# Ten gate tiles and the stick-breaking queries and keys of block 1 computed by 512-column products

## The chip, the cores and the metric

The program runs on one core of one Trainium2 chip. The metric is the device time of one execution in microseconds (us); lower is better. The core's engines work side by side, each through its own list of instructions in order: TensorE (PE, with its weight loads as PEld), VectorE (DVE), ScalarE (ACT), GpSimd (POOL) and SyncE (SP, which issues nearly all the transfers here).

## The reference

Two transformer blocks follow each other on 256 tokens of width 2048, in float32. The change lies in the first one. What it computes, cut to what matters:

```python
h = rms_norm(x, norm_g)
proj = h @ w_in                       # 2048 -> 8192
qa, ka, va, ga, qb, kb, vb, gb = split(proj)      # 1024 columns each
# stick-breaking attention, 8 heads of 128, blocks of 128 queries
z = (qa_head @ ka_head.T) * 128 ** -0.5
log_stay = where(s < t, log_sigmoid(-z), 0)
after = reversed_cumsum(log_stay) - log_stay
w = where(s < t, exp(log_sigmoid(z) + after), 0)
ya_head = w @ va_head
# yb: chunk-band attention on qb, kb, vb (8 heads)
mixed = concat([ya * silu(ga), yb * silu(gb)])
x = x + mixed @ w_out
```

The second block (latent attention, window attention and a convolutional feed-forward network of width 5632) is not touched.

## The kernel before

**Numbers in two parts.** A float32 operand of a large product is split into two tiles of the matrix type: `hi`, its rounded value (ACT), and `lo`, the rest (DVE, input minus `hi`). A product of weights and activations is then three: whi·ahi, whi·alo, wlo·ahi. Activations stand transposed, 256 tokens in the free direction, so a group of three for one block of 128 input features has three moving operands of 256 columns; this is `wmm` (L267 to L272). The second block's up projection has another form, `wide` (L274 to L278): there ahi and alo lie side by side in one tile, whi·[ahi alo] is one product of 512 columns into a whole PSUM bank, wlo·ahi one of 256 columns into its left half, and the two halves are added when the bank is emptied (L1553, L1554). For a block of 128 features `wmm` has three weight loads and 768 columns, `wide` two weight loads and 768 columns.

**The stream.** `Stream` holds a list of chunks of weights, 1024 columns each, which is 8 blocks of 128. SP loads a chunk, ACT makes `whi` (L123), DVE makes `wlo` (L125), and PE multiplies. There are four buffers for `whi` and four for `wlo`: the split of a chunk waits until PE has done with the chunk four places earlier. Rows of the second block's `ada` matrix go through the same stream; each is one DVE instruction (L392) of 1024 columns.

**The order.** The orders of PE and SP are those in which the code is written. Each chunk ticks a clock twice, once before its products and once after half of them, and tasks on it (`spawn`, `step`, `tick`) put their next instructions there. The orders of ACT and DVE are made by the scheduler when the program is built. Every engine then keeps its order, whatever comes ready first.

**The part that changes.** `x_pair` makes 16 pairs `hx` of activation tiles. `first_gates` and `w_pair` compute 16 gate tiles, each 128 output columns by 256 tokens, two to a bank; `gate_handler` multiplies them by `rrep`, each token's reciprocal norm (L618, DVE), and applies Silu (ACT). The first four tiles share two banks of tag `s`. The other twelve are six pairs, four chunks each, in banks of tag `g`, of which there are three, taken in turn. Much later come the eight stick-breaking heads: for each, `w_pair` makes the queries and the keys in one bank (four chunks), and `stick_head` empties it with one DVE instruction into `qkT` (L764). Two ticks later, in the middle of the next chunk, PE multiplies queries and keys (L767, L768; "the scores" below), and DVE takes the result (L770). The sums over later positions (L781 to L783) of the head before stand in PE's order directly behind the bank's last product; their result is taken by L784.

Of the kernel before, what the change touches and what calls it, by code (L numbers as in the profile page):

```python
# [9 lines left out]
F32 = mybir.dt.float32  # L10
F32R = mybir.dt.float32r
I32 = mybir.dt.int32
AF = mybir.ActivationFunctionType
ALU = mybir.AluOpType

P = 128
T = 256
# [197 lines left out]
def two_blocks(ctx, tc, xT, cvec, cst, vecs, w1, wo1, bch, ada, wz, wv, wuq, wuk, wuv, bsw, wo2, wup, wdn, out):  # L215
# [3 lines left out]
    def pool(name, side=None):  # L219
        kw = {} if side is None else {"side": side}  # L220
        return tc.alloc_tile_pool(name=name, bufs=1, reuse_waits="tile", **kw)
# [5 lines left out]
    S = Stream(tc, wp)  # L227
# [9 lines left out]
    def C(name):  # L237
        o, w = CST[name]
        if o < NCST0:
            return cs0[:, o:o + w]  # L240
        if o < NCST1:
            return ns["cs1"][:, o - NCST0:o - NCST0 + w]
        return cs[:, o - NCST1:o - NCST1 + w]

    def V(name, a=0, b=None):
        o, w = VEC[name]
        return vv[:, o + a:o + (w if b is None else b)]
# [3 lines left out]
    def bank(tag):  # L251
        t = psum.tile([P, 512], F32, tag=tag, name=tag, bufs={"g": 3, "s": 2, "t": 2, "o": 1}[tag])
        return t

    def two(ap):
        return ap.rearrange("p (a t) -> p a t", a=2)

    def act(**kw):
        return nc.scalar.activation(**kw)

    tt = nc.vector.tensor_tensor
# [4 lines left out]

    def wmm(out, whi, wlo, a, first, last):  # L267

        ahi, alo = a
        mm(out, lhsT=whi, rhs=ahi, start=first, stop=False)  # L270
        mm(out, lhsT=whi, rhs=alo, start=False, stop=False)  # L271
        mm(out, lhsT=wlo, rhs=ahi, start=False, stop=last)  # L272

    def wide(out, whi, wlo, a, first, last):  # L274

        ahi, alo, both = a
        mm(two(out), lhsT=whi, rhs=both, start=first, stop=False)  # L277
        mm(out[:, :T], lhsT=wlo, rhs=ahi, start=False, stop=last)  # L278

    def wchunk(lst):  # L280

        def mms(hi, lo):
            def one(c, e):
                out, a, first, last = e() if callable(e) else e
                wmm(out, hi[:, c * P:(c + 1) * P], lo[:, c * P:(c + 1) * P], a, first, last)
            return [lambda c=c, e=e: one(c, e) for c, e in enumerate(lst)]
        return mms
# [65 lines left out]
    def at_once(gen):  # L353
        try:
            while True:
                next(gen)
        except StopIteration as e:
            return e.value
# [52 lines left out]
    def ada_rate(r, upto):  # L411

        ada_acc[1:] = [r, upto]
# [47 lines left out]
    ph = pool("ph", "right")  # L461
    pmx = pool("pmx")
    p1 = pool("p1")
    hx = []
# [5 lines left out]
    def x_pair(q):  # L470
        if q % 2 == 0:
            tag = ("qt", "kt", "v", "v")[q // 2]
            t = p1.tile([P, 2, 512], F32, tag=tag, name="x4", bufs=3 if tag == "v" else 1)
            x4.append(t.rearrange("p a (k t) -> p (a k) t", t=T))
        xq = x4[q // 2][:, 2 * (q % 2):2 * (q % 2) + 2]
        for j in range(2):
            if j == 0 or q == 0:
                n = 1 if q == 0 else 2
                nc.sync.dma_start(out=xq[:, j:j + n], in_=xT[:, 2 * q + j:2 * q + j + n, :])
                if q == 0:  # L480
                    S.load_to(j + 1)
            hi = ph.tile([P, T], F32R, tag="hx", name="hx", bufs=32)
            lo = ph.tile([P, T], F32R, tag="hx", name="hx", bufs=32)
            g = V("ng", 2 * q + j, 2 * q + j + 1)
            ns["hx"] = act(out=hi, in_=xq[:, j], func=AF.Copy, scale=g)
            stt(out=lo, in0=xq[:, j], scalar=g, in1=hi.bitcast(F32), op0=ALU.mult, op1=ALU.subtract)
            hx.append((hi, lo))
            if q == 0:
                with tc.issue_after(ns["hx"].ins):
                    S.split_one()  # L490

    rt = p1.tile([P, 2], F32, name="rt")
    rrep = p1.tile([P, T], F32, name="rrep")
    rrep2 = rrep.unsqueeze(1).to_broadcast([P, 2, T])
# [24 lines left out]
    def w_pair(srcs, acts, handler, n=16, per=8, tag="g"):  # L519

        box = {}
        flat = [(a, k) for a in range(2) for k in range(n)]
        for c in range(0, 2 * n, per):
            part = flat[c:c + per]

            def pre():
                box["ps"] = bank(tag)

            def entry(a, k):
                return lambda: (box["ps"][:, a * T:(a + 1) * T], acts()[k], k == 0, k == n - 1)  # L530
            S.chunk(srcs(c // per), len(part) * P, wchunk([entry(a, k) for a, k in part]),
                    pre=pre if c == 0 else None,
                    post=(lambda: handler(box["ps"])) if c + per >= 2 * n else None)

    def w_one(srcs, acts, handler, n=16, per=8):
        box = {}
# [59 lines left out]
    hxs = lambda: hx  # L596
    u = [0]

    def next_w1(n):
        b = u[0]  # L600
        u[0] += n
        return lambda c: w1[b + c]


    order = list(range(8, 16)) + list(range(8))
    gates = {}

    def gate_handler(j):
        def h(ps):
            at_once(evac(ps))  # L610

        def late(ps):
            S.spawn(evac(ps), 8)

        def evac(ps):
            for i in range(2):
                gt = pmx.tile([P, T], F32, tag="mh", name="gate", bufs=16)
                tt(out=gt, in0=ps[:, i * T:(i + 1) * T], in1=rrep, op=ALU.mult)  # L618
                last = act(out=gt, in_=gt, func=AF.Silu)
                gates[order[2 * j + i]] = gt  # L620
            if j == 7:
                with tc.issue_after(last.ins):
                    nc.scalar.preload_act_table_set("natural_log_exp_and_others")
            yield 1
        return evac if j < 2 else late if j == 2 else h


    gb = []
# [23 lines left out]
    for j in range(2, 8):  # L652
        if j == 2:
            ada_rate(0.52, 64)
        w_pair(next_w1(4), hxs, gate_handler(j))

    mixed = {}

# [100 lines left out]

    SB = (2,1,4,2,1,3)  # L760

    def stick_head(ps, h):
        qk = p1.tile([P, 512], F32, tag="qkT", name="qkT", bufs=2)
        tt(out=two(qk), in0=two(ps), in1=rrep2, op=ALU.mult)  # L764
        yield SB[0]
        sc = bank("s")
        mm(sc[:, 0:256], lhsT=qk[:, 256:384], rhs=qk[:, 0:256], start=True, stop=True)  # L767
        mm(sc[:, 256:384], lhsT=qk[:, 384:512], rhs=qk[:, 128:256], start=True, stop=True)  # L768
        zm = p1.tile([P, 384], F32, tag="zm", name="zm", bufs=2)
        stt(out=zm, in0=sc[:, :384], scalar=128.0 ** -0.5, in1=C("msb"), op0=ALU.mult, op1=ALU.add)  # L770
        yield SB[1]
        e = p1.tile([P, 384], F32, tag="e", name="e", bufs=3)
        act(out=e, in_=zm, func=AF.Abs)
        act(out=e, in_=e, func=AF.Exp, scale=-1.0)
        act(out=e, in_=e, func=AF.Ln, bias=1.0)
        yield SB[2]
        sp = p1.tile([P, 384], F32, tag="sp", name="sp", bufs=2)
        stt(out=sp, in0=zm, scalar=0.0, in1=e, op0=ALU.max, op1=ALU.add)
        yield SB[3]
        cum = bank("s")  # L780
        mm(cum[:, 0:256], lhsT=C("tri"), rhs=sp[:, 0:256], start=True, stop=False)  # L781
        mm(cum[:, 128:256], lhsT=ones, rhs=sp[:, 256:384], start=False, stop=True)
        mm(cum[:, 256:384], lhsT=C("tri"), rhs=sp[:, 256:384], start=True, stop=True)  # L783
        tt(out=zm, in0=zm, in1=cum[:, :384], op=ALU.subtract)  # L784
        yield SB[4]
        w = p1.tile([P, 384], F32, tag="pT", name="pT", bufs=2)
        act(out=w, in_=zm, func=AF.Exp)
        yield SB[5]
        o = bank("o")
        hs = slice((h % 4) * 128, (h % 4 + 1) * 128)  # L790
        vt = qkv["va%d" % (h // 4)]
        attend(o, vt[:, 0, hs], vt[:, 1, hs], w)
        yield from finish_head(o, h)

    last_head = []
    for h in range(8):
        def handler(ps, h=h):
            t = S.spawn(stick_head(ps, h))
            S.step(t)
            last_head.append(t)  # L800
        w_pair(next_w1(4), hxs, handler)


    warm = small.tile([P, 2], F32, name="warm")
# [70 lines left out]
    for n, (j, a, hf) in enumerate(seq):  # L875
# [4 lines left out]
        def pre(j=j, a=a, hf=hf):  # L880
            if j not in banks1:
                banks1[j] = bank("g")
            if hf == 1 and "pu" not in ns:
                start_u()

        def entry(j, a, i):
            return lambda: (banks1[j][:, a * T:(a + 1) * T], mixed[order[i]], i == 0 and a == 0, i == 15 and a == 1)
        S.chunk(wo1[(2 * j + a) * 2 + hf], 1024, wchunk([entry(j, a, hf * 8 + i) for i in range(8)]), pre=pre,
                post=(lambda j=j: out1_handler(j)) if (a, hf) == (1, 1) else None)
# [864 lines left out]
```

## Time and profile before

| | us |
|---|---|
| median of 3 runs | 1886.03 |
| lowest and highest | 1885.96, 1886.21 |
| the profiled execution's own time | 1886.98 |
| its span in the trace | 1885.2 |

The profile is of one execution. Its span runs from the first to the last instruction of the program; about 1.8 us of the execution's own time lie around it. Engines' busy times overlap. A matmul's bar in the trace is longer than its share of PE, because matmuls are pipelined: the cost of one is the distance from its start to the start of the next. In the rows, "idle before" is how long an engine stood still before an instruction and the name behind the arrow is what ended it.

### The profile page before, as it was taken

The page shows a single profiled execution, that of the slowest core. Times are in us where ns is not written, and L with a number is a line of the kernel's source. Part 1 is how long each engine was busy: PE and PEld are TensorE (multiplying, and loading weights), DVE is VectorE, ACT ScalarE, POOL GpSimd, SP SyncE. Part 2 cuts the span into 40 slices and gives each one's busy share as a digit, 9 for nine tenths or more (in the row PEclk, how much of TensorE's full clock was granted, in tenths as well). Part 3 has the DMA queues.
Part 4 walks back from the last instruction along what each step waited for, and adds up shares of the span by engine and source line. Part 5 has one row for each costly group of instructions (what it writes and reads, how often), then busy time and mean ns, then how long its engine had stood idle before and what let it go on. Part 6 is the DMA issues. An engine that isn't in the chain of part 4 may idle for free.

```text
span 1885.2 us, 31970 instructions
## 1 busy us (share of the span) xinstructions
PE 1873.0 (99%) x12144; PEld 1704.0 (90%) x12144; DVE 1360.2 (72%) x2219; ACT 1015.4 (54%) x1650; POOL 188.6 (10%) x298
## 2 busy tenths in 40 slices
PE   9999999999999999999999999999999999999998
PEld 9988889999999999999999889888888888888886
DVE  7777877767787777777878766988888777644444
ACT  7445454444565555555566558555555555543442
POOL 0001120000125233330022100000000000000000
PEclk9999999999999999999999999999999999999999
DMA  9888777658688777768655664877777666656663
GB/s 357 300 278 298 248 264 262 239 188 266 196 302 278 256 256 265 261 209 270 214 175 176 236 223 160 266 245 251 249 247 245 191 190 190 190 179 190 190 190 123
DMA packets 128169, 438.92 MB, mean 233 GB/s; under 512 B 14352, under 2 KB 20368, under 8 KB 127760
## 3 DMA queue, kind: packets, MB, share of 16 engines
q1 hardware_dynamic: 127872, 436.88, 70.3%
q8 instruction: 95, 1.56, 0.3%
q14 instruction: 58, 0.48, 0.1%
q10 hardware_dynamic: 144, 0.01, 0.0%
HBM read 434.73 MB, written 2.10 MB: 232 GB/s over the span
## 4 chain that ended last, share of the span: by engine, by line
PE 97%; ACT 1%; DVE 1%; DMA 0%; POOL 0%; issue 0%; SPq 0%; DVEq 0%; POOLq 0%
PE g L277 16%; PE g L270 12%; PE g L272 12%; PE g L271 12%; PE g L278 8%; PE g L294 7%; PE g L295 7%; PE g L293 7%; PE s L293 3%; PE s L294 3%; PE s L295 3%; PE o L457 1%; PE t L450 1%; PE s L1132 1%; PE o L458 1%; PE s L272 1%
## 5 line engine op out<-in xcount | busy, mean ns | idle before, releaser
L125 DVE TENSOR_TENSOR wlo<-raw,whi 128x1024 fp32r<-128x1024 f32 (+2 forms) x623 | 762.6, 1225 | 383.8 <-ACT whi L123 376.1
L123 ACT ACTIVATE whi<-raw 128x1024 fp32r<-128x1024 f32 (+2 forms) x623 | 652.1, 1049 | 615.0 <-PE g L271 145.9
L277 PE MATMUL g<-h,whi 128*128 128x512 f32 x1344 | 466.1, 392 | 0.0
L278 PE MATMUL g<-h,wlo 128*128 128x256 f32 x1344 | 376.3, 280 | 0.0
L277 PEld LDWEIGHTS g<-h,whi 128*128 128x128 f32 x1344 | 252.3, 188 | 56.4
L270 PE MATMUL g<-h,whi 128*128 128x256 f32 x880 | 253.0, 288 | 0.0
L278 PEld LDWEIGHTS g<-h,wlo 128*128 128x128 f32 x1344 | 252.7, 188 | 0.0
L272 PE MATMUL g<-h,wlo 128*128 128x256 f32 x880 | 247.2, 281 | 0.0
L271 PE MATMUL g<-h,whi 128*128 128x256 f32 x880 | 247.2, 281 | 0.0
L392 DVE SCALAR_TENSOR_TENSOR raw<-raw,crep 128x1024 f32<-128x1024 f32 x192 | 239.0, 1245 | 1.6 <-DMA raw<-in_ada_dram 1.2
L271 PEld LDWEIGHTS g<-h,whi 128*128 128x128 f32 x880 | 166.0, 189 | 0.0
L270 PEld LDWEIGHTS g<-h,whi 128*128 128x128 f32 x880 | 166.0, 189 | 0.0
L272 PEld LDWEIGHTS g<-h,wlo 128*128 128x128 f32 x880 | 165.8, 188 | 0.0
L270 PE MATMUL g<-hx,whi 128*128 128x256 f32 x448 | 127.7, 285 | 0.0
L272 PE MATMUL g<-hx,wlo 128*128 128x256 f32 x448 | 125.8, 281 | 0.0
L271 PE MATMUL g<-hx,whi 128*128 128x256 f32 x448 | 125.8, 281 | 0.0
L293 PE MATMUL g<-whi,hx 128*128 128x512 f32 x256 | 104.6, 409 | 0.0
L295 PE MATMUL g<-whi,hx 128*128 128x512 f32 x256 | 101.0, 395 | 0.0
L294 PE MATMUL g<-wlo,hx 128*128 128x512 f32 x256 | 101.0, 395 | 0.0
L270 PEld LDWEIGHTS g<-hx,whi 128*128 128x128 f32 x448 | 84.5, 189 | 0.1
L271 PEld LDWEIGHTS g<-hx,whi 128*128 128x128 f32 x448 | 84.5, 189 | 0.1
L272 PEld LDWEIGHTS g<-hx,wlo 128*128 128x128 f32 x448 | 84.4, 188 | 0.0
(344 smaller groups left out, 3520.0 us busy)
## 6 DMA issues: line engine op xcount, KB each, us to landing
raw<-in_ada_dram SPq DMA_DIRECT2D x192, 512.0 KB, 4.4
raw<-in_wup_dram SPq DMA_DIRECT2D x176, 512.0 KB, 4.3
raw<-in_w_dram SPq DMA_DIRECT2D x127, 512.0 KB, 4.8
raw<-in_wz_dram SPq DMA_DIRECT2D x122, 512.0 KB, 4.6
raw<-in_wdn_dram SPq DMA_DIRECT2D x88, 512.0 KB, 3.6
raw<-in_wo_dram SPq DMA_DIRECT2D x64, 512.0 KB, 4.1
raw<-in_wuq_dram SPq DMA_DIRECT2D x24, 384.0 KB, 3.7
raw<-in_wuv_dram SPq DMA_DIRECT2D x8, 512.0 KB, 4.5
```

The source lines that it names most:

```text
L123: nc.scalar.activation(out=hi[:, :n], in_=raw, func=AF.Copy)
L125: last = nc.vector.tensor_tensor(out=lo[:, :n], in0=raw, in1=hi[:, :n].bitcast(F32), op=ALU.subtract)
L270: mm(out, lhsT=whi, rhs=ahi, start=first, stop=False)
L271: mm(out, lhsT=whi, rhs=alo, start=False, stop=False)
L272: mm(out, lhsT=wlo, rhs=ahi, start=False, stop=last)
L277: mm(two(out), lhsT=whi, rhs=both, start=first, stop=False)
L278: mm(out[:, :T], lhsT=wlo, rhs=ahi, start=False, stop=last)
L293: mm(out, lhsT=ahi[:, t], rhs=hi[:, w], start=first, stop=False)
L294: mm(out, lhsT=ahi[:, t], rhs=lo[:, w], start=False, stop=False)
L295: mm(out, lhsT=alo[:, t], rhs=hi[:, w], start=False, stop=last)
L392: stt(out=raw, in0=raw, scalar=1.0, in1=crep_now[0][:, h * 1024:(h + 1) * 1024], op0=ALU.mult, op1=ALU.mult, accum_out=modh[:, k:k + 1])
L450: nc.tensor.transpose(pt[:, j * P:(j + 1) * P], e[:, j * P:(j + 1) * P], ident)
```

## The change

The two parts of `hx` become the halves of one tile. A new `w_side` computes one output tile over two chunks by `wide`, in a bank of its own. A new `halves` empties such a bank: ACT copies its right half, DVE adds the left half to that. Of the six gate pairs, the first stays with `w_pair` and the other five become ten tiles of `w_side`, each emptied by ACT copy, DVE add, DVE multiplication by `rrep` and ACT Silu. The queries and the keys of a stick-breaking head become two `w_side` tiles; each is copied, added and multiplied into its half of `qkT`. The number and the order of chunks, and the ticks, are as before; so are the chunk-band products and values, which read `hx` as weights.

```diff
     def wmm(out, whi, wlo, a, first, last):
-        ahi, alo = a
+        ahi, alo = a[:2]
...
-            hi = ph.tile([P, T], F32R, tag="hx", name="hx", bufs=32)
-            lo = ph.tile([P, T], F32R, tag="hx", name="hx", bufs=32)
+            both = ph.tile([P, 2, T], F32R, tag="hx", name="hx", bufs=16)
+            hi, lo = both[:, 0], both[:, 1]
...
-            hx.append((hi, lo))
+            hx.append((hi, lo, both))
...
+    def w_side(srcs, acts, handler):
+        box = {}
+        for c in range(2):
+            def pre():
+                box["ps"] = bank("g")
+            def mms(hi, lo, c=c):
+                def one(j):
+                    k = c * 8 + j
+                    wide(box["ps"], hi[:, j * P:(j + 1) * P], lo[:, j * P:(j + 1) * P], acts()[k], k == 0, k == 15)
+                return [lambda j=j: one(j) for j in range(8)]
+            S.chunk(srcs(c), 1024, mms, pre=pre if c == 0 else None,
+                    post=(lambda: handler(box["ps"])) if c == 1 else None)
+
+    def halves(dst, ps):
+        act(out=dst, in_=ps[:, T:], func=AF.Copy)
+        tt(out=dst, in0=ps[:, :T], in1=dst, op=ALU.add)
...
+    def side_gate(i):
+        def h(ps):
+            gates[order[i]] = gt = pmx.tile([P, T], F32, tag="mh", name="gate", bufs=16)
+            halves(gt, ps)
+            tt(out=gt, in0=gt, in1=rrep, op=ALU.mult)
+            last = act(out=gt, in_=gt, func=AF.Silu)
...
     for j in range(2, 8):
-        w_pair(next_w1(4), hxs, gate_handler(j))
+        if j == 2:
+            w_pair(next_w1(4), hxs, gate_handler(j))
+        else:
+            for i in (2 * j, 2 * j + 1):
+                w_side(next_w1(2), hxs, side_gate(i))
...
-    def stick_head(ps, h):
-        qk = p1.tile([P, 512], F32, tag="qkT", name="qkT", bufs=2)
-        tt(out=two(qk), in0=two(ps), in1=rrep2, op=ALU.mult)
+    def stick_head(qk, h):
         yield SB[0]
...
+        def handler(ps, h=h, a=0, box=box):
+            if a == 0:
+                box["qk"] = p1.tile([P, 512], F32, tag="qkT", name="qkT", bufs=2)
+            qk = box["qk"][:, a * T:(a + 1) * T]
+            halves(qk, ps)
+            tt(out=qk, in0=qk, in1=rrep, op=ALU.mult)
+            if a == 1:
+                t = S.spawn(stick_head(box["qk"], h))
+                S.step(t)
+                last_head.append(t)
+        for a in range(2):
+            w_side(next_w1(2), hxs, lambda ps, a=a, h=handler: h(ps, a=a))
```

The change also gives DVE and ACT another order. Three places follow; in each row stand line, operation, the tile written, behind `<-` the tiles read, and the written shape.

**The first head, DVE.** The order of before, from the split of the chunk ahead of the bank's end to the taking of the scores (`zm`):

```order
L125 TENSOR_TENSOR wlo<-raw,whi 128x1024
L764 TENSOR_TENSOR qkT<-g,rrep 128x512
L125 TENSOR_TENSOR wlo<-raw,whi 128x1024
L392 SCALAR_TENSOR_TENSOR raw,modh<-raw,crep 128x1024
L770 SCALAR_TENSOR_TENSOR zm<-s,cs_237 128x384
```

The same place in the changed kernel, for the second tile (the keys); L552 is the addition in `halves`, L830 the multiplication by `rrep`, L796 the taking of the scores:

```order
L125 TENSOR_TENSOR wlo<-raw,whi 128x1024 x2
L552 TENSOR_TENSOR qkT<-g,qkT 128x256
L392 SCALAR_TENSOR_TENSOR raw,modh<-raw,crep 128x1024
L830 TENSOR_TENSOR qkT<-qkT,rrep 128x256
L796 SCALAR_TENSOR_TENSOR zm<-s,cs_221 128x384
```

The emptying stood between two splits; now its addition stands behind both, and an `ada` row stands between its two halves.

**A later head, DVE and ACT.** DVE before, at the end of a later bank:

```order
L392 SCALAR_TENSOR_TENSOR raw,modh<-raw,crep 128x1024
L764 TENSOR_TENSOR qkT<-g,rrep 128x512
L125 TENSOR_TENSOR wlo<-raw,whi 128x1024
L784 TENSOR_TENSOR zm<-zm,s 128x384
L770 SCALAR_TENSOR_TENSOR zm<-s,cs_237 128x384
```

DVE now (L810 is what L784 was):

```order
L392 SCALAR_TENSOR_TENSOR raw,modh<-raw,crep 128x1024
L810 TENSOR_TENSOR zm<-zm,s 128x384
L552 TENSOR_TENSOR qkT<-g,qkT 128x256
L125 TENSOR_TENSOR wlo<-raw,whi 128x1024
L830 TENSOR_TENSOR qkT<-qkT,rrep 128x256
L796 SCALAR_TENSOR_TENSOR zm<-s,cs_221 128x384
```

The split that stood behind the emptying now stands inside it, and L810 ahead of it. ACT before, over one head (two splits, and behind them the exponentials of the head before and of this one):

```order
L259 ACTIVATE mh<-m 128x256
L123 ACTIVATE whi<-raw 128x1024 x2
L259 ACTIVATE pT<-zm 128x384
L259 ACTIVATE e<-zm 128x384
```

ACT now:

```order
L259 ACTIVATE qkT<-g 128x256
L259 ACTIVATE mh<-m 128x256
L123 ACTIVATE whi<-raw 128x1024 x2
L259 ACTIVATE qkT<-g 128x256
L259 ACTIVATE pT<-zm 128x384
L259 ACTIVATE e<-zm 128x384
```

The copies are new. That of the keys stands behind two splits, and the second of these waits for the end of the same chunk as the copy itself.

**The second and third gate pairs, DVE.** Before, from the multiplication of the first four gates on; `gate<-g` is the pair of L618 that empties the first bank of tag `g`:

```order
L618 TENSOR_TENSOR gate<-s,rrep 128x256 x4
L125 TENSOR_TENSOR wlo<-raw,whi 128x1024
L392 SCALAR_TENSOR_TENSOR raw,modh<-raw,crep 128x1024
L125 TENSOR_TENSOR wlo<-raw,whi 128x1024
L618 TENSOR_TENSOR gate<-g,rrep 128x256 x2
```

Now (L634 is what L618 was, L552 and L644 empty the first of the ten tiles):

```order
L552 TENSOR_TENSOR gate<-g,gate 128x256
L634 TENSOR_TENSOR gate<-s,rrep 128x256
L644 TENSOR_TENSOR gate<-gate,rrep 128x256
L634 TENSOR_TENSOR gate<-s,rrep 128x256
L125 TENSOR_TENSOR wlo<-raw,whi 128x1024
L392 SCALAR_TENSOR_TENSOR raw,modh<-raw,crep 128x1024
L125 TENSOR_TENSOR wlo<-raw,whi 128x1024
L634 TENSOR_TENSOR gate<-g,rrep 128x256 x2
```

The emptying of the first bank (the last row) now stands behind that of the second.

## Rows read from the trace of the kernel before

**Rows 1.** The page: engines' busy time; DVE's busy tenths in 40 slices of 47.1 us.

```profile
PE 1873.0 (99%) x12144; PEld 1704.0 (90%) x12144; DVE 1360.2 (72%) x2219; ACT 1015.4 (54%) x1650; POOL 188.6 (10%) x298
...
DVE  7777877767787777777878766988888777644444
```

**Rows 2.** Products reading `hx`, 56.6 to 101.6 us: count, durations in ns, first and last start.

```profile
L270 PE MATMUL g<-hx,whi x128: 277/280/285, 56.4 to 101.5; 128*128 128x256 f32 x128
```

**Rows 3.** The same view for tile `h` (up projection), 1170 to 1629 us.

```profile
L277 PE MATMUL g<-h,whi x1325: 392/392/392, 1169.8 to 1628.7; 128*128 128x512 f32 x190
```

**Rows 4.** Timeline of PE from 120 us: start us, duration us, engine, line, operation, tiles.

```profile
120.00 0.39 PE L293 MATMUL g<-whi,hx 128*128 128x512 f32 x1
...
122.80 0.39 PE L293 MATMUL g<-whi,hx 128*128 128x512 f32 x1
```

**Rows 5.** Timeline around the end of the first stick-breaking bank.

```profile
308.81 1.06 ACT L123 ACTIVATE whi<-raw 128x1024 fp32r<-128x1024 f32 x1 [1.77 <-PE g L271]
...
308.94 0.69 DVE L764 TENSOR_TENSOR qkT<-g,rrep 128x512 f32<-128x512 f32 x1 [0.64 <-PE g L272]
...
309.91 1.23 DVE L125 TENSOR_TENSOR wlo<-raw,whi 128x1024 fp32r<-128x1024 f32 x1 [0.28 <-ACT whi L123]
...
310.15 0.59 PE L767 MATMUL s<-qkT 128*128 128x256 f32 x2
...
311.05 1.22 DVE L392 SCALAR_TENSOR_TENSOR raw<-raw,crep 128x1024 f32<-128x1024 f32 x1
...
312.19 0.55 DVE L770 SCALAR_TENSOR_TENSOR zm<-s,cs 128x384 f32<-128x384 f32 x1
```

**Rows 6.** Timeline around the end of the third stick-breaking bank.

```profile
334.27 0.59 PE L781 MATMUL s<-sp,cs 128*128 128x256 f32 x2
334.35 1.06 ACT L123 ACTIVATE whi<-raw 128x1024 fp32r<-128x1024 f32 x1 [1.78 <-PE g L271]
...
334.92 0.39 PE L783 MATMUL s<-sp,cs 128*128 128x128 f32 x2
...
335.50 1.22 DVE L125 TENSOR_TENSOR wlo<-raw,whi 128x1024 fp32r<-128x1024 f32 x1
...
336.56 0.59 PE L767 MATMUL s<-qkT 128*128 128x256 f32 x2
336.63 0.55 DVE L784 TENSOR_TENSOR zm<-zm,s 128x384 f32<-128x384 f32 x1
```

**Rows 7.** Timeline in the up projection, where a bank is emptied by halves.

```profile
1496.79 1.06 ACT L123 ACTIVATE whi<-raw 128x1024 fp32r<-128x1024 f32 x1 [1.27 <-issue]
...
1497.76 0.36 ACT L259 ACTIVATE z<-g 128x256 f32<-128x256 f32 x1
1497.89 1.23 DVE L125 TENSOR_TENSOR wlo<-raw,whi 128x1024 fp32r<-128x1024 f32 x1 [0.68 <-ACT whi L123]
...
1499.03 0.42 DVE L1554 TENSOR_TENSOR z<-g,z 128x256 f32<-128x256 f32 x1
```

**Rows 8.** Timeline of DVE and ACT among the gates.

```profile
50.81 1.07 ACT L123 ACTIVATE whi<-raw 128x1024 fp32r<-128x1024 f32 x1 [0.25 <-PE g L271]
...
57.04 0.75 DVE L618 TENSOR_TENSOR gate<-g,rrep 128x256 f32<-128x256 f32 x2
```

**Rows 9.** Timeline of PE: waits near the start, and one at 1041 us.

```profile
10.24 0.38 PE L270 MATMUL s<-hx,whi 128*128 128x256 f32 x1 [0.88 <-ACT whi L123]
...
11.50 0.39 PE L272 MATMUL s<-hx,wlo 128*128 128x256 f32 x1 [0.76 <-DVE wlo L125]
...
1041.86 0.44 PE L450 MATMUL t<-cs,e 128*128 128x128 f32 x2 [0.77 <-POOL e L443]
```

**Rows 10.** Windows: us; busy (instructions) of PE, PEld, DVE, ACT, POOL; granted clock; DMA share; GB/s.

```profile
12.00:14.00 2.00, 2.00 (x15) 2.00 (x14) 1.83 (x3) 1.47 (x3) 0.00 (x0) 0.68 1.05 422
14.00:16.00 2.00, 2.00 (x11) 2.00 (x11) 1.64 (x4) 1.89 (x4) 0.00 (x0) 0.50 1.03 413
1040.00:1044.00 4.00, 3.23 (x17) 2.54 (x16) 3.17 (x8) 2.41 (x7) 2.55 (x3) 1.00 0.91 286
```

More of the change, by code (lines that the diff above doesn't have):

```diff
@@ L608, in gate_handler @@
     def gate_handler(j):
-        def h(ps):
-            at_once(evac(ps))
         def late(ps):
@@ L618, in evac @@
                 tt(out=gt, in0=ps[:, i * T:(i + 1) * T], in1=rrep, op=ALU.mult)
-                last = act(out=gt, in_=gt, func=AF.Silu)
+                act(out=gt, in_=gt, func=AF.Silu)
                 gates[order[2 * j + i]] = gt
-            if j == 7:
+            yield 1
+        return evac if j < 2 else late
+    def side_gate(i):
[4 more added lines that the diff above has]
+            last = act(out=gt, in_=gt, func=AF.Silu)
+            if i == 15:
                 with tc.issue_after(last.ins):
                     nc.scalar.preload_act_table_set("natural_log_exp_and_others")
-            yield 1
-        return evac if j < 2 else late if j == 2 else h
+        return h
     gb = []
@@ L796, in two_blocks @@
     for h in range(8):
[L797 to L801, printed above, removed]
+        box = {}
+        def handler(ps, h=h, a=0, box=box):
[10 more added lines that the diff above has]
+            w_side(next_w1(2), hxs, lambda ps, a=a, h=handler: h(ps, a=a))
     warm = small.tile([P, 2], F32, name="warm")
```

## The prediction

> **What bounds the kernel now.** I read the busy times first: PE 99% of the span, DVE 72%, ACT 54% [rows 1]. So a change gains only where PE gets through its list sooner, and loses where PE is made to wait. A matmul's bar overlaps the next, so the cost of a product has to be read from starts; I looked for one stretch of each form with nothing else between, and divided. Then the timeline around the places where a bank that the change touches is emptied and PE soon needs the result [rows 5, 6, 8], since a longer way out of the bank costs nothing unless PE stands at its end. Last I looked for waits of PE and what the clock did behind them [rows 9, 10].
>
> **The products.** Ten gate tiles and sixteen query and key tiles have 16 blocks of features each: 26 x 16 = 416 groups. A group of three products costs (101.5 - 56.4) / 127 = 355.1 ns [rows 2]. A group of one wide and one narrow product costs (1628.7 - 1169.8) / 1324 = 346.6 ns in the up projection [rows 3], the same shapes and types. The difference, 8.5 ns, times 416 is **3.5 us gained**, all on PE. The lower bound: products of 512 columns in block 1 come every (122.80 - 120.00) / 12 = 233 ns [rows 4], there with weights as the moving side. If the wide product kept that pace and the narrow one a third of 355, a group would cost 351.7 ns and the gain be 3.4 x 416 = 1.4 us. I take 3.5, since [rows 3] is the very same pair.
>
> The Trainium skill, "TensorE: Matmul & The Clock Gate", section "Back-to-back issue gap", gives columns / 2.4 + 2.5 ns for one product, so a group would go from 327.5 to 325.0 ns and the gain be 1.0 us; by that the sum below would come out 2.5 us higher. The trace differs from it in both forms, 355.1 and 346.6, and the measured rows decide.
>
> **The heads' scores: a new wait of PE.** PE's order asks for the scores four groups behind a bank's last product, and they need the keys out of the bank. In before that is one DVE instruction. In the first head it runs from 308.94 to 309.63 and the scores start at 310.15, so 0.52 us were left [rows 5]; nothing waits. Now it is copy (ACT), addition and multiplication (DVE), and by the new orders other work stands in between. I count from s, the start of the split on ACT that the same chunk's end releases (308.81 and 334.35).
>
> A later head. ACT's copy stands behind that split. In the up projection such a copy starts 0.97 us behind the split's start and takes 0.36 [rows 7], so it ends at s + 1.33. L810 stands ahead of the addition on DVE; it needs the sums' last product, which starts at 334.92 and takes 0.39 [rows 6], so it can start at about s + 1.0, and with 0.5 us for it (0.55 less the overlap with the next) the addition starts at s + 1.5 and frees DVE at s + 1.85 (0.75 for two such in a row [rows 8]). Then comes the split: 1.14 from its start to the next instruction's (1497.89 to 1499.03 [rows 7]). So the multiplication starts at s + 3.0, ends at s + 3.4 (0.42), and the scores start some 0.15 later, for the signal and their weight load: s + 3.55. PE asks for them at 336.56 - 334.35 = 2.21 [rows 6], now 2.18 because the four groups are shorter. The wait is **1.4 us** (an estimate from these rows; I bound it by 1.0 and 1.7). All seven later heads have this order: 7 x 1.4 = 9.6 us.
>
> The first head has no sums ahead of it, but the split on DVE comes first, starting at s + 1.10 and lasting to s + 2.24 [rows 5]; addition to s + 2.6; the `ada` row, 311.05 to 312.19 = 1.14 [rows 5], to s + 3.75; multiplication to s + 4.15; scores at s + 4.3. PE asks at 310.15 - 308.81 = 1.34. The wait is **3.0 us** (bounds 2.4 and 3.4). While PE waits in its order, every product behind the scores waits too; the splits have four buffers and go on, so nothing is caught up later. The heads lose 12.6 us together.
>
> **The clock.** Near the start PE stood idle for 0.88 and 0.76 us within 2.4 us [rows 9], and shortly behind that the granted clock was 0.68 of 2.4 GHz over 12 to 14 us and 0.50 (1.2 GHz) over 14 to 16 [rows 10]: 2 x 0.32 + 2 x 0.50 = 1.6 us lost. Behind the wait of 0.77 us at 1041 us it stayed at 1.00 [rows 9, 10]. A wait of 3.0 us is longer than both of the first together, so I charge the first head **1.6 us** (bounds 0 and 1.6). Waits of 1.4 lie between the cases, about as near to 0.77 as to the 1.64 that the two at the start make together; each stands alone, and I charge them nothing and keep 7 x 1.6 = 11.2 us as a rival.
>
> **The gates.** The ten tiles are emptied with time to spare, three banks in turn and 5.5 us to a tile, save one place: the first bank of tag `g` is wanted again by the third of the ten tiles, and on DVE its emptying now stands behind that of the first of them. The split at 50.81 [rows 8] is released by the end of the second chunk behind the first pair; these two chunks took 16 x 355.1 ns = 5.68 us [rows 2], so that pair ends at 45.1, and two chunks of 16 x 346.6 ns = 5.55 us now end at 50.7. Copy and signal: 51.15. Addition and three multiplications at 0.35: 52.55. Split, `ada` row, split, 1.14 each: 56.0. The two multiplications, 0.75 [rows 8]: 56.75. PE wants the bank four chunks behind 45.1, at 56.1 (a product starts about 0.1 ahead of that release). A wait of **0.7 us** (bounds 0 and 1.2).
>
> **What costs nothing.** ACT gets 26 copies of about 0.4 us, DVE some 26 additions and a multiplication more for each head. The cover is the four buffers of the splits: a split is released three chunks, some 8 us, before its chunk is needed, and takes 1.06 + 1.23. Near the gates two copies stand ahead of a split that is released one chunk earlier, so this one starts 2.8 us late and still ends 2 us before it is needed. In the up projection DVE is 80 to 90% busy [rows 1] and PE's pace there is even [rows 3]. If the cover failed, each late split would cost up to 1 us. Loads, GpSimd and SP's queue keep their orders; the new joint tile for `hx` only alters the order of the first 25 us, where the splits' loads set the pace and the same two waits remain.
>
> **The sum.** -3.5 + 9.6 + 3.0 + 1.6 + 0.7 = **+11.4 us**: the span goes from 1885.2 to 1896.6, the profiled execution's own time from 1886.98 to 1898.4; against the median of the runs, 0.05% lower than that execution, 1886.03 + 11.4 = **1897.4 us**.
>
> **The rivals.**
>
> *The scores find their operands ready.* One mechanism on the other side, at the scores' place in PE's order: if multiplication ends by s + 2.0, PE never waits there and the products' 3.5 us remain, less the gates' 0.7: 1883.2 us. It speaks for it that copy, addition and multiplication alone take only about 1.2 us, and that without the split between them they would end at s + 2.3, a wait of 0.25 per head. Against it: the order on DVE is fixed when the program is built, and a split of the same kind holds the addition in the up projection in the same way, from 1497.89 to 1499.03 though the copy was there at 1498.12 [rows 7]. It decides from the point where the multiplication stands ahead of the split.
>
> *The clock falls behind every head's wait.* Then seven times 1.6 us come on top: 1908.6. For it speaks the sum of the waits at the start, against it the 1.00 at 1041 us [rows 9, 10]. In between lie cases where it falls behind some of them.
>
> *The wide products bring little in this place* (the change does not do what it says): 1.4 us instead of 3.5, with the waits as above, 1899.5.
>
> *The waits are shorter than I make them*, because the scheduler's order happens to meet idle DVE time that I do not see: 0.7 per later head, 1.5 in the first, clock untouched: -3.5 + 4.9 + 1.5 + 0.7 = +3.6, 1889.6.
>
> **How the numbers follow.** Forecast (1893 to 1902) 0.60; clock falling behind some or all of the seven waits 0.16; little from the wide products 0.06, inside the forecast's range; shorter waits 0.10; operands ready 0.08. The bounds of the single terms, without the seven falls, give -3.5 + 7.0 + 2.4 + 0 + 0 = +5.9 and -1.4 + 11.9 + 3.4 + 1.6 + 1.2 = +16.7. With half of the falls the upper end is about 1908. The range is 1890 to 1908: it leaves out the operands-ready case, half of the shorter waits and a little at the top. A measurement of this kernel can tell about 0.2% from no change, here 3.8 us. Operands ready lies at 2.8 us and counts as no change, with 0.02 left for a gain of over 3.8; of the shorter waits half lies within it. So faster 0.02, same 0.11, slower 0.87.
>
> **What would show it.** In the profile of the changed kernel: 346 to 347 ns from one wide product on `hx` to the next; PE idle ahead of the first score product of each head, about 1.4 us in seven of them and 3 us in the first, ended by DVE's multiplication into `qkT`, which starts directly behind a split; a clock below 1.00 behind the first head and nowhere else among the heads; one wait of under 1.2 us at about 56 us, ended by a multiplication into a gate. I am wrong if the scores start without a wait, if the pace of the wide products is that of [rows 2], or if PE waits for `whi` or `wlo` among the heads.

## The result and the profile after

| | us |
|---|---|
| before, median of 4 executions | 1885.99 |
| after, median of 4 (1898.30 to 1905.93) | 1899.91 |
| ratio, 95% interval | 1.0078 (1.0066 to 1.0089) |
| after, the profiled execution and its span | 1900.28, 1898.5 |

The change makes the kernel 13.9 us slower; 11.4 were forecast. One execution of the kernel before, in a later series, lay in another state at 3972.67 us and stands in no comparison. From the page of the changed kernel: the span, and the busy times that answer to [rows 1].

```profile
span 1898.5 us, 31186 instructions
...
PE 1875.2 (99%) x11728; PEld 1684.9 (89%) x11728; DVE 1369.7 (72%) x2253; ACT 1021.9 (54%) x1676; POOL 194.1 (10%) x298
```

PE has 416 matmuls and weight loads fewer than in [rows 1], as wanted, but its busy time is no shorter and the span is 13.3 us longer. The waits of PE, grouped by what it waited for (total us, times, longest), name the new one:

```profile
PE s L793 <- DVE qkT L830: 10.6, 8, 2.7
PE s L270 <- ACT whi L123: 1.5, 1, 1.5
```

The first line is not there in the kernel before: eight waits at the scores for the multiplication into `qkT`. The second is 0.9 us there, near the start; the first product into a bank of tag `g` starts at the same time all the same, 32.73 us against 32.77 before. The timeline of a later head (start us, duration us, engine, line; in brackets idle time and what ended it) shows the chain behind it:

```profile
340.78 1.06 ACT L123 ACTIVATE whi<-raw 128x1024 fp32r<-128x1024 f32 x1 [1.71 <-PE g L277]
...
341.74 0.37 ACT L259 ACTIVATE qkT<-g 128x256 f32<-128x256 f32 x1
341.77 0.55 DVE L810 TENSOR_TENSOR zm<-zm,s 128x384 f32<-128x384 f32 x1 [0.30 <-PE s L809]
342.24 0.42 DVE L552 TENSOR_TENSOR qkT<-g,qkT 128x256 f32<-128x256 f32 x1
...
342.58 1.22 DVE L125 TENSOR_TENSOR wlo<-raw,whi 128x1024 fp32r<-128x1024 f32 x1
...
342.87 0.28 PE L278 MATMUL g<-hx,wlo 128*128 128x256 f32 x1
343.71 0.42 DVE L830 TENSOR_TENSOR qkT<-qkT,rrep 128x256 f32<-128x256 f32 x1
344.27 0.67 PE L793 MATMUL s<-qkT 128*128 128x256 f32 x2 [1.13 <-DVE qkT L830]
```

From the split's start on ACT, s = 340.78: copy at s + 0.96, addition at s + 1.46, split on DVE at s + 1.80, multiplication at s + 2.93, scores at s + 3.49. The product ahead of the scores starts at 342.87, so PE stands still for more than its bar shows: 1.41 us from start to start in place of 0.12, **1.29 us lost**. The first head loses 2.97 - 0.12 = **2.85 us** (309.64 to 312.61). PE's starts there, and at the second head:

```profile
309.64 0.28 PE L278 MATMUL g<-hx,wlo 128*128 128x256 f32 x1
312.61 1.22 PE L793 MATMUL s<-qkT 128*128 128x256 f32 x2 [2.69 <-DVE qkT L830]
...
329.59 0.67 PE L793 MATMUL s<-qkT 128*128 128x256 f32 x2 [1.14 <-DVE qkT L830]
```

Behind the first head the clock falls. Windows of 2 us (busy time and instructions of PE, PEld, DVE, ACT, POOL; granted clock; DMA share; GB/s):

```profile
310.00:312.00 2.00, 0.00 (x0) 0.00 (x0) 2.00 (x3) 0.00 (x0) 0.00 (x0) 0.96 0.72 279
312.00:314.00 2.00, 1.39 (x5) 1.21 (x5) 0.56 (x3) 0.00 (x0) 0.00 (x0) 0.50 0.34 53
314.00:316.00 2.00, 2.00 (x9) 1.71 (x8) 0.56 (x1) 1.02 (x2) 0.00 (x0) 0.50 1.00 395
316.00:318.00 2.00, 2.00 (x8) 1.71 (x8) 0.27 (x1) 1.38 (x3) 0.00 (x0) 0.50 0.23 84
318.00:320.00 2.00, 2.00 (x11) 1.73 (x11) 1.43 (x2) 0.11 (x1) 0.00 (x0) 0.83 0.00 0
```

PE does nothing from 310 to 312, then works at 0.50 of 2.4 GHz, that is 1.2 GHz, until some time past 318. From the first head's scores to the second's it takes 16.98 us (312.61 to 329.59); before, 12.89 (310.15 to 323.04). Less the second head's own wait, 1.29, that is **2.8 us** for the clock.

Where the ten tiles run, the row of the wide product (count, first and last start) answers to [rows 2] and [rows 3]:

```profile
L277 PE MATMUL g<-hx,whi x160: 392/396/402, 45.0 to 101.1; 128*128 128x512 f32 x160
```

(101.1 - 45.0) / 159 = 352.8 ns for a group, not the 346.6 of [rows 3]. Single starts, PE alone, show how:

```profile
59.79 0.39 PE L277 MATMUL g<-hx,whi 128*128 128x512 f32 x1
60.02 0.28 PE L278 MATMUL g<-hx,wlo 128*128 128x256 f32 x1
60.14 0.40 PE L277 MATMUL g<-hx,whi 128*128 128x512 f32 x1
60.38 0.28 PE L278 MATMUL g<-hx,wlo 128*128 128x256 f32 x1
60.50 0.39 PE L277 MATMUL g<-hx,whi 128*128 128x512 f32 x1
```

Every other group is longer: 346 ns (229 + 117), then 361 (240 + 121). In the up projection of the same execution the groups take 346.6. I call these the uneven and the even pace.

### The profile page after: what moved, and what is told of

Its sections match the earlier page's. It is cut to its first block, busy times and chain, and to the rows that moved or that the text cites. A ratio compares the mean times of both kernels' runs of the same rounds, so it can differ in the third digit from the quotient of the medians.

```text
span 1898.5 us, 31186 instructions
## 1 busy us (share of the span) xinstructions
PE 1875.2 (99%) x11728; PEld 1684.9 (89%) x11728; DVE 1369.7 (72%) x2253; ACT 1021.9 (54%) x1676; POOL 194.1 (10%) x298
## 4 chain that ended last, share of the span: by engine, by line
PE 96%; DVE 2%; ACT 1%; DMA 0%; issue 0%; POOL 0%; SPq 0%; DVEq 0%; POOLq 0%
PE g L277 21%; PE g L278 11%; PE g L270 9%; PE g L272 9%; PE g L271 9%; PE g L294 7%; PE g L293 7%; PE g L295 7%; PE s L295 3%; PE s L294 3%; PE s L293 3%; PE o L457 1%; PE t L450 1%; PE s L1167 1%; DVE wlo L125 1%; PE o L458 1%
## 5 line engine op out<-in xcount | busy, mean ns | idle before, releaser
L277 PE MATMUL g<-hx,whi 128*128 128x512 f32 x416 | 151.2, 404 | 0.0
L278 PE MATMUL g<-hx,wlo 128*128 128x256 f32 x416 | 117.9, 283 | 0.0
L277 PEld LDWEIGHTS g<-hx,whi 128*128 128x128 f32 x416 | 79.3, 191 | 18.5
L443 POOL TENSOR_TENSOR e<-e,st 128x128 f32<-128x128 f32 x112 | 68.1, 628 | 121.5 <-DVE st L439 110.7
L278 PEld LDWEIGHTS g<-hx,wlo 128*128 128x128 f32 x416 | 79.5, 191 | 0.0
L270 PE MATMUL g<-mh,whi 128*128 128x256 f32 x256 | 72.5, 283 | 0.0
```

The source lines that it names most:

```text
L443: nc.gpsimd.tensor_tensor(out=es, in0=es, in1=st[:, 6 + c:7 + c].to_broadcast([P, w]), op=ALU.mult)
```

## Experiments

The theory after the comparison: the loss arises at the heads (11.9 us of waits and 2.8 of clock), and the products gain next to nothing. Rivals: the wide products or the gates take part in the loss; the emptying is too long in itself, whatever stands inside it; the clock's fall belongs to the place of the first head.

**The gates alone.** Gates as after, heads as before:

```diff
-    def stick_head(qk, h):
+    def stick_head(ps, h):
+        qk = p1.tile([P, 512], F32, tag="qkT", name="qkT", bufs=2)
+        tt(out=two(qk), in0=two(ps), in1=rrep2, op=ALU.mult)
...
-        for a in range(2):
-            w_side(next_w1(2), hxs, lambda ps, a=a, h=handler: h(ps, a=a))
+        w_pair(next_w1(4), hxs, handler)
```

> The ten gate tiles as in the change, the heads as before. Theory (the whole loss arises at the heads): no wait of PE over 0.3 us between 33 and 110 us, the stretch of the gates 0.3 us shorter than before as in the changed kernel, the heads as before; the time within 1.5 us of before, 1884.5 to 1886. By the terms of the prediction: 160 groups x 8.5 ns = 1.4 us gained and 0.7 us lost to a wait at 56 us, 1885.3. Rival (the wide products or their emptying cost something in this place): slower than before by over 2 us.

Measured: 12 executions, five from 1884.59 to 1887.14 and seven from 1893.60 to 1897.15, none between; before, beside it, 28 with a median of 1886.2, none over 1889.45. The median, 1893.65, lies far above the range expected, beyond the 2 us of the rival; the ratio of the means is 1.0022 (1.0007 to 1.0037). In the traced one (1894.04), PE's stretch from the first product into a bank of tag `g` to the last score of the heads is 0.3 us shorter than in the kernel before, with no wait in it. A loss of 8.6 us arises later, in the up projection, which no part of the change touches:

```profile
L277 PE MATMUL g<-h,whi x1247: 392/392/402, 1189.6 to 1629.9; 128*128 128x512 f32 x179
```

Now (1629.9 - 1189.6) / 1246 = 353.4 ns a group: the uneven pace, 6.8 ns more for each of nearly 1300 groups. It begins with a short disturbance at 1181.8 us and then keeps itself up:

```profile
1181.48 0.39 PE L277 MATMUL g<-h,whi 128*128 128x512 f32 x1
1181.70 0.28 PE L278 MATMUL g<-h,wlo 128*128 128x256 f32 x1
1181.82 0.40 PE L277 MATMUL g<-h,whi 128*128 128x512 f32 x1
1182.06 0.30 PE L278 MATMUL g<-h,wlo 128*128 128x256 f32 x1
1182.20 0.40 PE L277 MATMUL g<-h,whi 128*128 128x512 f32 x1
```

From 1182.06 to 1182.20 are 140 ns in place of 117. The traces show what comes ahead of it. This is the first group of a chunk, and DVE has only just made its `wlo`, because ACT, further ahead, had to wait for the load of `crep`, the factor of the `ada` rows. PEld is the load of the group's `wlo` as weights:

```profile
1171.58 1.91 ACT L259 ACTIVATE crep<-crep 128x2048 f32<-128x2048 f32 x1 [0.88 <-DMA crep<-in_cvec_dram]
...
1180.69 1.22 DVE L125 TENSOR_TENSOR wlo<-raw,whi 128x1024 fp32r<-128x1024 f32 x1
...
1181.97 0.19 PEld L278 LDWEIGHTS g<-h,wlo 128*128 128x128 f32 x1
```

The same three in the kernel before, where ACT does not wait and the pace stays even:

```profile
1172.15 1.92 ACT L259 ACTIVATE crep<-crep 128x2048 f32<-128x2048 f32 x1
...
1181.26 1.22 DVE L125 TENSOR_TENSOR wlo<-raw,whi 128x1024 fp32r<-128x1024 f32 x1
...
1183.28 0.19 PEld L278 LDWEIGHTS g<-h,wlo 128*128 128x128 f32 x1
```

Here the weight load starts 0.06 us behind the split's end and 0.15 behind the wide product; before, 0.80 behind the split's end and together with the wide product. All ten traces of this document fit. In each the split ends 10.3 us behind the start of that ACT instruction. Counted from the first wide product of the up projection, this split ends at 19.4 to 20.0 us in the six whose pace stays even, and at 20.25 to 20.39 in the three where it turns uneven, each time at this group. In one, the second trace of the changed kernel, it ends at 20.85; there PE waits 0.21 us and goes on evenly. So what stands ahead of the uneven pace is the landing of one load, which differs from execution to execution: for the changed kernel ACT waits 0 us for it in the first trace and 1.35 in the second. No run moved that load, so this is read off the traces and not tried.

The traced executions bear out that the two groups of times are the two paces of the up projection: even at 1886.23 (the kernel with transposes, below), uneven at 1894.04 here and at 1894.15 (the split behind the emptying). The gates cost nothing at their own place, and gain nothing that can be told. Whether this kernel meets the uneven pace more often stays open: seven of 12 executions here against none of the 28 beside it, but six of 23 of the kernel before in a later series. That the times would fall into two groups was not expected. The other kernels have to be read with this in mind.

**The heads alone.** Heads as after, gates as before (`w_pair` with `gate_handler(j)` for all six pairs).

> The heads as in the change, the gates as before. Theory: the same eight waits (2.7 us and seven of 1.3) and the clock at 1.2 GHz behind the first, 2.8 us: 11.9 + 2.8 = 14.7 us, less at most 2 for the products: 1898.5 to 1901. Rival (half of the loss belongs to the gates or to the joint tile of hx): under 1894.

Measured: 1897.88 (1897.27 to 1901.75), 11.6 us above before; ratio 1.0067 (1.0055 to 1.0080). The eight waits are those of the whole change to 0.02 us. In the traced execution, 1899.86, the clock cost 1.6 us behind the first head, not 2.8. From the first product into a bank of tag `g` to the last score, PE takes 13.6 us longer than before, against 14.3 in the whole change: the loss is the heads'. The median is 0.6 below the range; a clock that costs less in some executions would explain it, which no trace shows.

**The scores one tick later.**

```diff
-    SB = (2,1,4,2,1,3)
+    SB = (3,1,4,2,1,3)
```

> The changed kernel with the scores one tick later in PE's order (the first number of SB 3 instead of 2), four groups or 1.4 us. Theory: seven waits of 1.3 us vanish and that of the first head falls from 2.7 to about 1.3 us, with the clock staying at 1.00 behind it: 9.0 + 1.4 + 2.8 = 13.2 us back, 1886 to 1888. If the first head's wait of 1.3 us still lets the clock fall: 1889. Rival (PE is held by something else, or the wait moves to the sums): over 1893.

Measured: 1886.53 (11 executions, 1886.26 to 1888.43). Two waits are left, 1.56 - 0.12 = 1.44 us in the first head and 0.67 in the second, and the clock stays at 1.00. Four groups of slack take the loss away: what was late was the operand of the scores, and nothing else came in its place.

**The split behind the emptying.** Nothing is left out of the chain and the scores keep their place:

```diff
-            halves(qk, ps)
-            tt(out=qk, in0=qk, in1=rrep, op=ALU.mult)
+            with tc.high_priority(0):
+                first = halves(qk, ps)
+                last = tt(out=qk, in0=qk, in1=rrep, op=ALU.mult)
+            S.gate = first, last
+            S.spawn(ungate(), 2)
```

`S.gate` lets the next chunk's `whi` follow the copy (`halves` now returns it) and its `wlo` the multiplication; `ungate` takes that back behind the next split. `high_priority` tells the scheduler how to rank the emptying, so the edit gives it two hints at once.

> The changed kernel with the next chunk's split put behind the emptying on both engines: whi behind the copy on ACT, wlo behind the multiplication on DVE. Theory (the split inside the emptying is the wait): no wait at the scores (multiplication ends about 1.9 us behind the chunk's end, scores are asked for at 2.2), clock 1.00 throughout the heads, 11.9 + 2.8 us back: 1884 to 1886. Rival A (copy, addition and multiplication are too long by themselves): waits of 0.3 us or more stay at each head, 1888 or more. Rival B (the later splits make PE wait for wlo): waits of about 1 us for wlo instead, 1893 or more.

Measured: ten executions with a median of 1887.3, 1.3 above the range expected, and two at 1894.2 and 1894.9 (the traced one among them: uneven pace in the up projection). Of the waits at the scores none is left. The same place in a later head:

```profile
332.62 0.42 DVE L552 TENSOR_TENSOR qkT<-g,qkT 128x256 f32<-128x256 f32 x1
...
333.01 0.55 DVE L815 TENSOR_TENSOR zm<-zm,s 128x384 f32<-128x384 f32 x1
333.48 0.42 DVE L836 TENSOR_TENSOR qkT<-qkT,rrep 128x256 f32<-128x256 f32 x1
...
333.81 1.22 DVE L125 TENSOR_TENSOR wlo<-raw,whi 128x1024 fp32r<-128x1024 f32 x1
334.22 0.59 PE L798 MATMUL s<-qkT 128*128 128x256 f32 x2
```

The scores start with no idle time ahead. Rival A falls: copy, addition and multiplication fit, and the split between them was the wait. Rival B holds at one place, behind the last head's bank, where PE waits 0.5 us for `whi` and 1.1 for `wlo`, about what the time lies above the range; among the heads it does not.

**The changed kernel again**, unaltered.

> The changed kernel once more, beside the others of this call. In the kernel with only the gates changed the up projection went at 346.6 ns for a group in some executions and at 353.4 in others, 8.6 us apart. Theory (which of the two a stream of wide products takes is a state that it enters, and not a matter of the code): executions near 1899 and some near 1908, none between 1903 and 1906. Rival (noise of another kind): an even spread.

Measured: 1898.30 (1895.92 to 1899.56, 6 executions), none near 1908, so the second group of times was not met here; the one execution at 1905.93 of the first comparison could be one with the uneven pace, but was not traced. The trace shows something else. The first head's wait is again 2.85 us, but the clock does not fall:

```profile
310.00:312.00 2.00, 0.10 (x1) 0.00 (x0) 2.00 (x3) 0.00 (x0) 0.00 (x0) 1.00 0.79 324
312.00:314.00 2.00, 1.21 (x7) 1.12 (x8) 0.99 (x4) 0.00 (x0) 0.00 (x0) 1.00 0.33 55
```

PE's starts are 2.6 us ahead of those in the first trace at the last score, and 1.3 us at the last matmul: 0.8 are lost again in the `wmm` products behind the heads and 0.5 at the late `wlo` of the up projection.

**Longer waits.** In the handler of head h, behind the multiplication of the keys:

```diff
+            for _ in range(h if a == 1 else 0):
+                tt(out=qk, in0=qk, in1=qk, op=ALU.max)
```

> The changed kernel with h more DVE instructions (maximum of a tile with itself, about 0.34 us each) behind the multiplication of head h, so that the waits grow: 2.7 us in head 0 and about 1.6, 2.0, 2.3, 2.6, 3.0, 3.3 and 3.6 in heads 1 to 7; 28 x 0.34 = 9.4 us more of waits. Theory (a long wait is what lets the clock fall, wherever it stands): the granted clock stays at 1.00 behind the short ones and falls below 1.00 behind those as long as the first head's, four to six falls of 1.6 to 2.8 us, 1899.9 + 9.4 + 6.4 to 16.8 = 1916 to 1926. Rival (the place of the first head is what counts, behind a long stretch without a wait): the clock stays at 1.00 in all later heads, 1909.

Measured: 1934.02 and 1927.77, both above the range. The waits came out longer than laid out, because in heads 1 and 5 an `ada` row, 1.14 us, got in between. The first product of the scores in heads 0 to 7, with PE's idle time ahead:

```profile
312.85 1.22 PE L793 MATMUL s<-qkT 128*128 128x256 f32 x2 [2.69 <-DVE qkT L830]
330.00 1.19 PE L793 MATMUL s<-qkT 128*128 128x256 f32 x2 [2.62 <-DVE qkT L832]
347.04 0.67 PE L793 MATMUL s<-qkT 128*128 128x256 f32 x2 [2.05 <-DVE qkT L832]
363.26 0.69 PE L793 MATMUL s<-qkT 128*128 128x256 f32 x2 [2.51 <-DVE qkT L832]
381.35 1.19 PE L793 MATMUL s<-qkT 128*128 128x256 f32 x2 [2.96 <-DVE qkT L832]
400.77 0.67 PE L793 MATMUL s<-qkT 128*128 128x256 f32 x2 [4.45 <-DVE qkT L832]
419.78 1.19 PE L793 MATMUL s<-qkT 128*128 128x256 f32 x2 [3.89 <-DVE qkT L832]
440.24 1.19 PE L793 MATMUL s<-qkT 128*128 128x256 f32 x2 [4.33 <-DVE qkT L832]
```

Windows behind the third and the fourth of them:

```profile
347.00:349.00 2.00, 1.96 (x11) 1.80 (x12) 0.56 (x1) 0.38 (x1) 0.00 (x0) 1.00 0.62 240
364.00:366.00 2.00, 2.00 (x8) 1.71 (x8) 0.56 (x1) 0.97 (x2) 0.00 (x0) 0.50 0.15 59
```

Behind 2.05 us the clock stays at 1.00; behind each of the seven from 2.51 up it falls to 0.50. So the fall is not bound to the place of the first head, and the rival falls. It went with the length of the wait in this trace; but behind the wait of 2.69 us in the second trace of the changed kernel there was none, so the length alone does not settle it. Of the 47 us by which its last matmul is later than before, 26.8 are these waits and some 8.6 the uneven pace of the up projection; the other 12 or so belong mostly to the seven falls, about 1.7 us each (worked out as the rest, not measured singly).

**Transposes ahead of the gates.** The kernel with the gates alone, and ahead of the first of the ten tiles:

```diff
+                if kick:
+                    t = bank("t")
+                    for b in range(8):
+                        nc.tensor.transpose(t[:, b % 4 * P:(b % 4 + 1) * P], ident, ident)
                 box["ps"] = bank("g")
```

> The kernel with only the gates changed, and eight transposes (0.87 us of PE) ahead of the first of the ten tiles, as they stand near the start of the up projection. Theory (the slow pace of the gates is a state that the stream carries in from the wmm products ahead, and products of another form end it): 346.6 ns for a group in all ten tiles, the gates 160 x 6.8 = 1.1 us shorter, less 0.87. Rival A (something about hx or this place makes it slow): 353.4 ns as before. The up projection is expected in either of its paces in both cases: executions near 1885 and near 1894.

Measured: nine executions with a median of 1886.5 and three from 1893.4 to 1895.4; before, beside it, 17 near 1886.8 and six from 1894.4 to 1897.3, so the unchanged kernel meets both times too. All ten tiles now go evenly:

```profile
L277 PE MATMUL g<-hx,whi x160: 392/392/480, 44.7 to 99.9; 128*128 128x512 f32 x160
```

(99.9 - 44.7) / 159 = 347.2 ns. Same products, same operands, same place: rival A falls, and which pace the tiles take depends on what stands ahead of them. Whether it is the other form of the transposes or the break that they make in the stream was not separated, and what the pace is within PE, the traces don't show.

**A version with both.** The split behind the emptying for the keys of heads 0 to 6, the last head's scores one tick later, and the eight transposes.

> The changed kernel with the split behind the emptying, for the keys of the first seven heads alone, the last head's scores one tick later, and the eight transposes ahead of the ten tiles. Theory: no wait at the scores over 0.3 us, none for wlo behind the heads, the clock at 1.00 among the heads, the wide products of gates and heads at 346.6 ns where the transposes and score products end the slow state: 1882.5 to 1885 when the up projection goes at its fast pace, 8.7 us more when it does not. Rival (the emptying still comes late in some heads): 1886 or more at the fast pace.

Measured: ten executions with a median of 1883.6 (1883.10 to 1886.93) and two at 1892.4 and 1893.4. All taken together the ratio is 0.9988 (0.9973 to 1.0002); like against like (ten against the 17 near 1886.8) it is 3.3 us faster than before. No wait at the scores or among the heads is left; the gates and six of the eight heads go evenly, the first two unevenly. By these times it beats both kernels, by 0.17% where the up projection is taken to go evenly; over all executions the interval still holds no change. Its traced execution, 1886.93, is the slowest of the ten: its last matmul starts only 0.3 us ahead of that of the kernel before, with a wait of 0.85 us at 882 us that the kernel before does not have. How the others gain more, no trace shows.

## Why the prediction was right, and where it was off

The forecast's mechanism at the heads holds, and the size of the sum: 1899.9 measured, 1897.4 forecast. That the sum came so near is in part luck, since misses of single terms cancel. The terms, in the first traced execution, from the shift of PE's starts against the kernel before (the shift of its last matmul is 13.4 us):

| term | forecast us | measured us |
|---|---|---|
| products | -3.5 | -0.3 |
| seven later heads | +9.6 | +9.0 |
| first head | +3.0 | +2.85 |
| clock | +1.6 | +2.8 |
| gates' wait | +0.7 | 0 |
| not foreseen: `wmm` products behind the heads | | -0.9 |

The products brought 3.2 us less and the clock cost 1.2 more than forecast; the heads, the gates and the last row together came out 2.4 lower.

*The heads* came as worked out, step for step: multiplication at s + 2.93 (forecast 3.0), scores at s + 3.49 (3.55), first head's scores at s + 4.18 (4.3). That the order of the engine decides, and not the length of the emptying, was the ground of the forecast, and the split put behind confirms it: with it the operands are ready, as that rival demanded. No wait for `whi` or `wlo` came up among the heads. The cover of the splits was read a little too well for the up projection: the slices of [rows 1] show DVE 70 to 80% busy there from about 1460 us on, not 80 to 90%, and near its start one split can end so late that the pace suffers, 8.6 us and not the up to 1 us given for a late split.

*The products* were mis-sized: the step "I take 3.5, since [rows 3] is the very same pair" failed. The same pair has two paces, and [rows 3] shows the even one, while gates and most of the heads ran unevenly at 353. That is 1.7 ns a group below [rows 2], 0.7 us for 416 groups where my lower bound was 1.4; the starts show 0.3, at the gates, and nothing among the heads, where scores follow each other in 13.53 us before and in 14.83 with a wait of 1.29. So the rival that the wide products bring little held in this one term. The estimate worked out from the Trainium skill, "TensorE: Matmul & The Clock Gate", section "Back-to-back issue gap", 1.0 us, lies nearer to 0.3 than mine, but neither pace is its 325 ns.

*The clock* fell behind the first head alone, as forecast, and cost 2.8 us against a bound of 1.6; in two other traces of the same wait it cost 1.6 and nothing. The bound was read from one stretch at the start, and a single fall does not bound the next: in the kernel with transposes PE waits 0.86 and 0.76 us at that same place, and the granted clock stays at 1.00 from 12 to 16 us. The same page of the Trainium skill, section "Part 1: The HAM clock gate", says of the warm-up at a kernel's start that the number of slow matmuls varies between runs of one kernel. No run here counts those; what the traces show, 2.8, 1.6 and 0 us, is the like behind the first head, in the middle of the kernel.

*The gates.* The pair's bank is emptied at 55.98 to 56.73, as forecast (56.0 to 56.75), but the third tile starts at 56.26 with no wait. It has another bank then: the step "is wanted again by the third of the ten tiles" assumed that banks come in turn. DVE had taken the first tile out of its bank by 51.65, so the bank first released seems to be given out; that is inferred and was not tried.

*Not foreseen:* between 420 and 500 us the `wmm` products go at 360.0 ns a group before and 356.0 after, 0.9 us in the first trace's favour. They also have more than one pace, and this one belongs to the execution and not to the change: in the second trace of the changed kernel they go at 359.8 ns.

## What to carry to other kernels

When a result is emptied by several instructions, look up what the scheduler has put between them on each engine, and count to the last of them: a split of 1.14 us inside an emptying of 1.2 us cost 1.3 us a head. Move the consumer or the split, not the arithmetic. And take a product's price from the place where it will run: one stretch at an even pace is no promise for another.

## What was not expected of the hardware

- A stream of one wide and one narrow product with a weight load each has two steady paces, 346.6 and 353.4 ns a group. In three traces one group that was 4, 11 or 27 ns longer, behind a weight tile that came late, stood at the turn from the first to the second for the remaining 450 us (8.6 us); a wait of 0.21 us at the same group did not bring the turn. Eight transposes ahead of the ten gate tiles kept these from it. Which pace the up projection takes differed between executions, by the times of the unchanged program too (six of 23 executions near 1895).
- The clock's fall is not a fixed price: behind the same idle time of 2.69 us in the first head it cost 2.8 us, 1.6 us or nothing. Behind 2.05 us and less among the heads it was not seen; near the start, behind two waits of under 0.9 us, it came in one trace and not in another.
